# A hybrid decoder block on one core: a seeded accumulation bank, reordered key evacuation, later scaling of probabilities, and more weight tiles in flight

## The chip, the cores and the metric

The kernel runs on one core of one Trainium2 chip. The metric is device time in microseconds (us). Five engines work side by side, each through its own queue in order: TensorE (PE, with PEld for its weight loads), VectorE (DVE), ScalarE (ACT), GpSimd (POOL) and SyncE (SP). In this kernel SP and POOL only issue transfers from device memory, apart from a few fills on POOL. Products land in PSUM, eight banks of 128 x 512 float32. Everything else lies in SBUF.

## The reference, cut to what matters

Sequence 512, model width 1024, float32 throughout.

```
h = rmsnorm(x, norm1_w);  proj = h @ w_in[l]            # rq rk rv rg mq mk mv ga gb
ret = silu(rg) * retention(rotary(rq), rotary(rk)/sqrt(128), rv);  a = ret @ w_ret_out
mq, mk = per-head rmsnorm;  b = moba_attention(mq, mk, mv) @ w_moba_out
x = x + (sigmoid(ga) * a + sigmoid(gb) * b) @ w_o
f = (silu(h2 @ w_ffn_gate) * (h2 @ w_ffn_up)) @ w_ffn_down;  x + f     # h2 = rmsnorm(x, norm2_w), hidden 2816
```

With 512 keys in two blocks of 256 and three selected, the block-sparse attention is the ordinary causal softmax here: eight heads of width 64.

## The kernel before

Every product is made to float32 accuracy out of three passes: each operand is split into a rounded high part and the rest, and `mm3` adds high x high, high x low, low x high. For a weight tile of 128 x 1024 (`raw`) this means one cast on ACT (line 387, `wh<-raw`) and one subtraction on DVE (`wl<-raw,wh`; the helper that records DVE and PE operations is line 217, so their rows all carry L217).

Most of the work is cut into **units** of two output halves by two inner halves, done with seven block products in place of eight (the Winograd form of Strassen's scheme). The weight pieces are called B11, T1, T2, B21, B22, T3, T4, where T1 and T3 are differences that the transfers make, by an accumulating transfer on POOL (line 333) onto a tile that SP has loaded (line 331), and T2 and T4 are further sums: DVE adds them (`raw<-raw,raw`), except that in the units of w_o and of three of the four w_ffn_down parts T4 comes by another accumulating POOL transfer (line 357), which waits until DVE has split T2. The order of a unit is `B11 T1 *1 T2 B21 B22 T3 / T4`: the part behind the slash is put off into the next unit, where `*1` stands. Its banks are X (B11, then T2, T3 and T4 added onto it), Y (T1, B22) and Z (B21). What an `ev` object does with a bank as it goes:

- `p1`: after B11, ACT copies X to SBUF (lines 829 and 1534). T2 may write X only after that.
- `p5`, `u2`: ACT copies of Y and X with the sign turned.
- `c11`: after B21, DVE adds Z and the copy of `p1`: the first quarter of the result. One step later the quarter goes to its consumer (`out`), or in the hidden layer through SiLU on ACT.
- `c12`, `c22`, `c21`: the other quarters.

The banks come from one pool of eight (`main_ps`, `side_ps`), in rotation, for the units and for the side work alike: scores, transposes, values. SBUF tiles of 128 x 1024 come from a pool of 47 (`pairs`), also in rotation, so a tile is handed to its next user in the order in which tiles were given back.

**Order of work.** The emission is written out by hand. Each call of `advance` is a step (about one block of 12 products): first it runs what `later(n, f)` put off by n steps, then it ages the weight splits in flight, then it may start the next one, within a cap (`AHEAD`, `OAHEAD`, `FAHEAD`, `PAHEAD`) and by a running balance of DVE's and PE's load. `run_bg` then does one piece of side work from a list. An arriving weight tile is asked for when an earlier one has been used up (`used` calls `load_w`), so the number in flight stays the same, apart from `EXTRA` (before the values' unit of the attention) and `OEXTRA` (before the unit of w_o), which each add one.

**Stages.** Queries and keys (`tok_double`, four banks each, evacuated by `qk_evac`: copy, square on ACT and sum of squares on DVE, bank by bank; keys in banks 1 and 3 are copied by DVE), then the unit of mv, then gates and retention with the attention as side work (scores, `norm`, transposes, values), the two output branches, w_o, the second norm, and the FFN in four parts of 6, 6, 6 and 4 hidden tiles: units for gate and up, then one for w_ffn_down. The first hidden unit of the FFN is plain (eight products), the second has the order `B11 B21 T1 ...`.

In the attention, `norm` (reciprocal of the row sum and scaling of the probabilities, on DVE) is put off by NLAG = 1 step behind the exponential; the transposes follow four steps behind the scores.

Of the kernel before, what the change touches and what calls it, by code (L numbers as in the profile page):

```python
# [39 lines left out]
EXTRA = 1  # L40
OEXTRA = 1
ORDER = (("rg", 0), ("rk", 0), ("rv", 0), ("gb", 0), ("rk", 1), ("rv", 1), ("rg", 1), ("gb", 1), ("b", 0), ("b", 1), ("ga", 0), ("a", 0), ("ga", 1), ("a", 1))
# [10 lines left out]
ATT = (4, 6)  # L53
NLAG = 1
OAHEAD = (4, 6)
# [109 lines left out]
def hybrid_block(ctx: ExitStack, tc: tile.TileContext, wall, xin, xtok, n2, cin, out):  # L165
# [92 lines left out]
    def later(n, f):  # L258
        later_q.append([n, f])
# [55 lines left out]
    assert not left  # L315
    wstate = {"next": 0, "live": 0, "cap": AHEAD, "load": 0}
    wwait = []
# [20 lines left out]
    def used(r):  # L338

        uses[r] -= 1  # L340
        if not uses[r]:
            del raw[r]
            for f in load_w():
                f()

# [29 lines left out]
    def piece_emit():  # L375
        u, q = r = porder[wstate["next"]]
        wstate["next"] += 1
        wstate["live"] += 1
        fresh = r not in raw
        if fresh:  # L380
            make_sum(u, q)
        w = slice(0, width[r])
        src = raw[r][:, w]

        def high():
            h = big(nm("wh"), F32R)[:, w]
            A.copy(h, src)  # L387
            return h

        def low(h):  # L390
            l = big(nm("wl"), F32R)[:, w]
            V.tensor_tensor(l, src, h.bitcast(F32), ALU.subtract)
            was_split(r)
            return l

        p = Piece(high, low, HLAG if fresh else 0, LLAG)
        pieces[u, q] = p
        wwait.append(p)
# [269 lines left out]
    cur = [0]  # L668

    def tok_double(mov, evac):  # L670

        pss = [main_ps() for _ in range(NT)]
        lows = []
        for k in range(KT):
            for t in range(NT):
                m = ("A11", "A21", "A12", "A22")[k // 4 * 2 + t // 2]
                mm3(pss[t], tuple(x[:, t % 2 * P:t % 2 * P + P] for x in hW(m, k % 4)), mov(k), k == 0, k == KT - 1)
            advance(1)
            for l in lows:
# [78 lines left out]
    def wino_unit(w, ev, hooks={}):  # L758
# [7 lines left out]
        def bank(b):  # L766
            if b not in banks:
                banks[b] = [main_ps(), main_ps()] if wide else main_ps()
            return banks[b]

        def third(x):
            ev.c22(x)
            if "T4w" in order:
                ev.u3(x)

        whole = "T4w" in order
        table = {"B11": ("X", "A11", True, False, ev.p1), "T1": ("Y", "S1", True, False, ev.p5),
                 "T2": ("X", "S2", False, False, ev.u2), "B21": ("Z", "A12", True, True, ev.c11),
                 "B22": ("Y", "S4", False, True, ev.c12), "T3": ("X", "S3", False, whole, third),
# [42 lines left out]
    class Quarters:  # L822
# [4 lines left out]

        def p1(self, x):
            A.copy(self.a[:, :512], x)  # L829

# [6 lines left out]
        def c11(self, z):  # L837
            a = self.a[:, :512]
            V.tensor_tensor(a, z, a, ALU.add)
            later(1, lambda: self.out(0, 0, a))  # L840

# [21 lines left out]
    def qk_evac(i, tiles):  # L863
        def f(t, ps):

            if t % 2 == 0:
                tiles[t], tiles[t + 1] = halves(nm("qk"))
            sq = act(nm("sqh"))
            if i and t % 2:
                V.tensor_copy(tiles[t], ps)  # L870
            else:
                A.copy(tiles[t], ps)
            A.activation(sq, tiles[t] if i else ps, AF.Square)
            V.tensor_reduce(ss[:, i, t, :], sq.rearrange("p (h d) -> p h d", d=MDH), AX.X, ALU.add)
        return f
# [103 lines left out]

    for _ in range(EXTRA):  # L980
        for f in load_w():
            f()
    wino_unit(hW, Quarters(mv_out))


# [85 lines left out]
    def rg_unit(n):  # L1071
        def out(pair, i, x):
            if (pair, i) == (1, 0):
                A.copy(ev.free, x)
                x = ev.free
            srg[2 * n + i, pair] = x
            if (pair, i) == (1, 0):
                gates(n)
                ret_done("rg")

        ev = Quarters(out)
        wino_unit(hW, ev)
# [62 lines left out]
    def rv_out(h0):  # L1145
        def f(pair, i, x):
            rv[h0 + i, pair] = split(f"rv{h0 + i}_{pair}", x, None, 0 if (pair, i) == (1, 0) else SLAG[1])
            if (pair, i) == (1, 0):
# [363 lines left out]
    wstate["cap"] = OAHEAD  # L1512
    for _ in range(OEXTRA):
        for f in load_w():
            f()
    A.activation(warm, warm, AF.Sqrt)
# [8 lines left out]
    class Hidden:  # L1525
# [6 lines left out]

        def p1(self, x):
            A.copy(self.a0, x)

# [6 lines left out]
        def c11(self, z):  # L1542
            V.tensor_tensor(self.a0, z, self.a0, ALU.add)
            later(1, lambda: A.activation(self.a0, self.a0, AF.Silu))

# [64 lines left out]

    wstate["cap"] = FAHEAD
    for c in range(len(CHUNKS)):
        mats = {}
# [83 lines left out]
```

## Time and profile before

| | us |
|---|---|
| median of 3 runs | 813.05 |
| lowest, highest | 810.21, 813.63 |
| the profiled execution | 809.42 |
| its span, first to last instruction | 807.6 |
| PE busy | 783.9 (97%) |
| DVE busy | 659.3 (82%) |
| ACT busy | 438.6 (54%) |
| POOL busy | 64.1 (8%) |

The busy time of an engine is the union of its instructions. Matmuls are pipelined, so one shows 284 ns where the next starts 120 ns later. An idle time in a row of a timeline stands in brackets with what ended it. The share of DMA in a row of windows is the mean over the core's 16 DMA engines.

### The profile page before, as it was taken

How to read it: one execution, taken by the hardware profiler on the slowest of the kernel's cores; microseconds unless marked ns; L12 is line 12 of the kernel's file. 1: busy time of each engine (PE TensorE's matmuls, PEld its weight loads, DVE VectorE, ACT ScalarE, POOL GpSimd, SP SyncE). 2: the span in 40 equal slices, each digit the busy share in tenths (PEclk: the TensorE clock that was granted, in tenths of full speed). 3: DMA queues.
4: the chain of work that ended last, by engine and by line, in shares of the span. 5: the costliest groups of instructions: out<-in, count | busy, mean ns of one | idle time of the engine just before them, and what ended most of it. 6: DMA issues, size and time to landing. Idle time of an engine off the chain costs nothing.

```text
span 807.6 us, 13676 instructions
## 1 busy us (share of the span) xinstructions
PE 783.9 (97%) x5398; PEld 722.5 (89%) x5398; DVE 659.3 (82%) x996; ACT 438.6 (54%) x720; POOL 64.1 (8%) x84
## 2 busy tenths in 40 slices
PE   6998999999999999999999999999999999998997
PEld 5888988888999999998988798988999899987996
DVE  7869878777898678877678998886998798886987
ACT  8546755566537457653545575543555356552641
POOL 0004000000000000000001000011101110020100
PEclk9999999999999999999999999999999999999999
DMA  9742342333527637261798704569837795669702
GB/s 331 229 115 68 105 119 66 75 82 131 130 57 183 151 122 196 90 189 43 244 271 259 182 27 135 138 173 276 211 115 169 216 294 142 157 149 296 177 19 104
DMA packets 38080, 125.95 MB, mean 156 GB/s; under 512 B 4224, under 2 KB 4480, under 8 KB 38016
## 3 DMA queue, kind: packets, MB, share of 16 engines
q1 hardware_dynamic: 28800, 93.88, 33.8%
q0 software_dynamic: 9216, 31.20, 22.5%
q8 instruction: 42, 0.69, 0.3%
q14 instruction: 22, 0.18, 0.1%
HBM read 122.97 MB, written 2.10 MB: 155 GB/s over the span
## 4 chain that ended last, share of the span: by engine, by line
PE 66%; DVE 15%; DMA 7%; issue 7%; ACT 4%; POOL 1%; SPq 0%; ACTq 0%; DVEq 0%; POOLq 0%
PE pm L217 58%; PE ps L217 7%; DMA raw<-wall 7%; DVE wl L217 6%; ACT wh L387 2%; DVE xr L217 2%; DVE raw L217 2%; DVE h L217 1%; DVE ws L217 1%; DVE fb L217 1%; DVE qk L217 0%; ACT p L1007 0%; DVE mx L217 0%; POOL raw L357 0%; DVE gs L217 0%
## 5 line engine op out<-in xcount | busy, mean ns | idle before, releaser
L217 DVE TENSOR_TENSOR wl<-raw,wh 128x1024 fp32r<-128x1024 f32 (+1 forms) x224 | 258.2, 1168 | 44.2 <-ACT wh L387 36.1
L387 ACT CAST wh<-raw 128x1024 fp32r<-128x1024 f32 (+1 forms) x224 | 219.5, 1006 | 104.0 <-DVE raw L217 60.9
L217 PE MATMUL pm<-h,wh 128*128 128x256 f32 x1248 | 226.2, 284 | 3.5 <-ACT h L1467 1.0
L217 PEld LDWEIGHTS pm<-h,wh 128*128 128x128 f32 x1248 | 195.0, 192 | 5.3 <-ACT h L1467 1.2
L217 PE MATMUL pm<-h,wl 128*128 128x256 f32 x624 | 176.8, 283 | 1.1 <-DVE wl L217 1.1
L217 PEld LDWEIGHTS pm<-h,wl 128*128 128x128 f32 x624 | 119.7, 192 | 1.5 <-DVE wl L217 1.5
L333 POOL DMA_DIRECT2D raw<-wall x56 | 49.4, 885 | 636.8 <-DMA raw<-wall 238.9
L217 PE MATMUL pm<-hA,wh 128*128 128x256 f32 x448 | 83.0, 285 | 0.0
L217 PEld LDWEIGHTS pm<-hA,wh 128*128 128x128 f32 x448 | 70.1, 192 | 1.0 <-issue 0.5
L217 PE MATMUL pm<-wh,hA 128*128 128x256 f32 (+1 forms) x304 | 69.1, 310 | 0.0
L217 PE MATMUL pm<-wh,hS 128*128 128x256 f32 x320 | 64.3, 290 | 3.6 <-ACT qa L829 3.6
L217 PE MATMUL pm<-hA,wl 128*128 128x256 f32 x224 | 63.4, 283 | 1.7 <-DVE wl L217 1.7
L217 DVE TENSOR_TENSOR raw<-raw,raw 128x1024 f32<-128x1024 f32 (+1 forms) x48 | 57.0, 1187 | 0.8
L217 PEld LDWEIGHTS pm<-wh,hS 128*128 128x128 f32 x320 | 52.7, 195 | 4.1 <-ACT qa L829 3.8
L217 PEld LDWEIGHTS pm<-wh,hA 128*128 128x128 f32 x304 | 51.0, 191 | 2.5
L217 DVE TENSOR_TENSOR xr<-xr,pm 128x512 f32<-128x512 f32 x74 | 47.0, 679 | 1.3 <-PE pm L217 1.3
L217 PE MATMUL pm<-hS,wh 128*128 128x256 f32 x256 | 47.4, 285 | 0.0
L217 PE MATMUL pm<-wl,hA 128*128 128x256 f32 (+1 forms) x152 | 46.4, 305 | 0.0
L217 PE MATMUL pm<-wl,hS 128*128 128x256 f32 x160 | 45.7, 286 | 0.0
L217 PEld LDWEIGHTS pm<-hA,wl 128*128 128x128 f32 x224 | 42.9, 191 | 1.9 <-DVE wl L217 1.9
L217 PEld LDWEIGHTS pm<-hS,wh 128*128 128x128 f32 x256 | 40.0, 192 | 0.1
L217 PE MATMUL pm<-ret,wh 128*128 128x512 f32 x128 | 39.5, 390 | 0.0
(257 smaller groups left out, 1406.4 us busy)
## 6 DMA issues: line engine op xcount, KB each, us to landing
raw<-wall SPq DMA_DIRECT2D x153, 512.0 KB, 4.6
raw<-wall POOLq DMA_DIRECT2D x55, 512.0 KB, 6.6
raw<-wall SPq DMA_DIRECT2D x23, 256.0 KB, 4.4
raw<-wall POOLq DMA_DIRECT2D x9, 256.0 KB, 6.9
xr<-xtok SPq DMA_DIRECT2D x4, 512.0 KB, 7.9
out<-xr SPq DMA_DIRECT2D x8, 256.0 KB, 2.1
x<-xin SPq DMA_DIRECT2D x7, 256.0 KB, 5.4
cs<-cin SPq DMA_DIRECT2D x1, 512.0 KB, 5.5
```

What stands on the lines that cost most here:

```text
L217: return f(out, *args, **kw)
L333: nc.gpsimd.dma_start(t[:, s], wall[c, :, s], accum_op=ALU.add)
L387: A.copy(h, src)
```

## The change

It has six parts.

1. One bank, `zbank`, is taken out of the rotation for good and serves as Z of every unit (and as the last bank of the queries' product). In units whose order has T1 second and whose products are 256 wide (`seed`), `p1` has ACT copy X into Z instead of into SBUF, and B21 is accumulated onto it. `c11` then has no addition: the consumer reads Z.
2. Following from it, the quarter of `c11` goes out a step earlier, the retention's values are split at once, and the retention gate's unit copies the quarter to SBUF on ACT.
3. `qk_evac` copies all four banks first, and squares the copies after the last.
4. NLAG goes from 1 to 2.
5. `more_raws` replaces the loops that add weight tiles: OEXTRA goes from 1 to 5, and FEXTRA = -2 takes two back at the start of the FFN.
6. A weight piece of at most 512 columns puts its high and low parts in the two halves of one tile of the pool.

```diff
-OEXTRA = 1
+OEXTRA = 5
+FEXTRA = -2
...
-NLAG = 1
+NLAG = 2
...
         if not uses[r]:
             del raw[r]
-            for f in load_w():
-                f()
+            if wstate["drop"]:
+                wstate["drop"] -= 1
+            else:
+                for f in load_w():
+                    f()
+
+    def more_raws(n):
+
+        wstate["drop"] += max(-n, 0)
+        for _ in range(n):
+            if wstate["drop"]:
+                wstate["drop"] -= 1
+            else:
+                for f in load_w():
+                    f()
...
         def high():
-            h = big(nm("wh"), F32R)[:, w]
+            if width[r] <= 512:
+                both.extend(halves(nm("wh"), F32R))
+            else:
+                both.append(big(nm("wh"), F32R))
+            h = both[0][:, w]
...
+    zbank = main_ps()
+
     def tok_double(mov, evac):
 
-        pss = [main_ps() for _ in range(NT)]
+        pss = [main_ps() for _ in range(NT - 1)] + [main_ps() if cur[0] else zbank]
...
+                z = zbank if b == "Z" else main_ps()
+                banks[b] = [z, main_ps()] if wide else z
...
+        def first(x):
+            ev.p1(*([x, bank("Z")] if seed else [x]))
+
         whole = "T4w" in order
+        seed = not wide and order[1] != "B21"
...
-        def p1(self, x):
-            A.copy(self.a[:, :512], x)
+        def p1(self, x, z):
+            A.copy(z, x)
...
         def c11(self, z):
-            a = self.a[:, :512]
-            V.tensor_tensor(a, z, a, ALU.add)
-            later(1, lambda: self.out(0, 0, a))
+            self.out(0, 0, z)
...
             if t % 2 == 0:
                 tiles[t], tiles[t + 1] = halves(nm("qk"))
-            sq = act(nm("sqh"))
             if i and t % 2:
                 V.tensor_copy(tiles[t], ps)
             else:
                 A.copy(tiles[t], ps)
-            A.activation(sq, tiles[t] if i else ps, AF.Square)
-            V.tensor_reduce(ss[:, i, t, :], sq.rearrange("p (h d) -> p h d", d=MDH), AX.X, ALU.add)
+            if t == NT - 1:
+                for x in range(NT):
+                    sq = act(nm("sqh"))
+                    A.activation(sq, tiles[x], AF.Square)
+                    V.tensor_reduce(ss[:, i, x, :], sq.rearrange("p (h d) -> p h d", d=MDH), AX.X, ALU.add)
...
-            if (pair, i) == (1, 0):
-                A.copy(ev.free, x)
-                x = ev.free
+            if i == 0:
+                y = ev.free if pair else ev.a[:, :512]
+                A.copy(y, x)
+                x = y
...
-    for _ in range(OEXTRA):
-        for f in load_w():
-            f()
+    more_raws(OEXTRA)
...
         def c11(self, z):
-            V.tensor_tensor(self.a0, z, self.a0, ALU.add)
-            later(1, lambda: A.activation(self.a0, self.a0, AF.Silu))
+            if not self.whole:
+                V.tensor_tensor(self.a0, z, self.a0, ALU.add)
+                z = self.a0
+            A.activation(self.a0, z, AF.Silu)
...
     wstate["cap"] = FAHEAD
+    more_raws(FEXTRA)
```

## Rows read from the trace of the kernel before

**Rows 1.** PE's waits from 50 to 200 us: total, times, longest

```profile
PE pm L217 <- ACT qa L829: 3.6, 1, 3.6
PE pm L217 <- DVE wl L217: 2.1, 2, 1.7
PE ps L217 <- ACT pt L1039: 0.5, 1, 0.5
```

**Rows 2.** PE's waits from 502 to 790 us

```profile
PE pm L217 <- DVE xr L217: 2.1, 2, 1.9
PE pm L217 <- DVE wl L217: 1.3, 3, 0.8
...
PE pm L217 <- ACT wh L387: 0.5, 1, 0.5
```

**Rows 3.** Windows: stretch, busy time of PE, PEld, DVE, ACT, POOL (instructions), PEclk, DMA share, GB/s

```profile
61.30:65.10 3.80, 0.21 (x2) 0.00 (x1) 2.82 (x5) 3.04 (x5) 0.86 (x1) 0.93 0.30 37
65.10:68.10 3.00, 2.99 (x14) 3.00 (x15) 2.65 (x5) 1.32 (x3) 0.00 (x0) 0.52 0.73 143
68.10:72.00 3.90, 3.90 (x35) 3.90 (x34) 3.69 (x10) 2.79 (x4) 2.08 (x4) 1.00 0.00 0
104.90:106.90 2.00, 0.31 (x3) 0.11 (x2) 1.88 (x4) 0.59 (x3) 0.86 (x1) 1.00 0.51 172
421.00:460.00 39.00, 39.00 (x176) 32.12 (x175) 35.38 (x51) 19.95 (x33) 4.31 (x5) 1.00 0.92 238
```

**Rows 4.** ACT's timeline behind the keys: start, length, instruction [idle before, ended by]

```profile
56.34 0.59 ACT L872 COPY qk<-pm 128x512 f32<-128x512 f32 x1
...
62.06 0.63 ACT L873 ACTIVATE sqh<-qk 128x512 f32<-128x512 f32 x1 [1.35 <-DVE qk L217]
62.60 1.98 ACT L387 CAST wh<-raw 128x1024 fp32r<-128x1024 f32 x2
64.48 0.57 ACT L829 COPY qa<-pm 128x512 f32<-128x512 f32 x1
```

**Rows 5.** DVE's timeline behind the keys

```profile
58.23 0.68 DVE L217 COPY qk<-pm 128x512 f32<-128x512 f32 x1
...
63.66 1.22 DVE L217 TENSOR_TENSOR wl<-raw,wh 128x1024 fp32r<-128x1024 f32 x1 [0.25 <-ACT wh L387]
```

**Rows 6.** DVE's waits, from 62 to 107 us (first row) and from 107 to 200 us (second)

```profile
DVE rl L217 <- ACT p L1007: 3.6, 4, 1.3
...
DVE rl L217 <- ACT p L1007: 14.4, 17, 1.4
```

**Rows 7.** Groups of DVE by form: count, busy us, mean ns, idle before

```profile
L217 DVE TENSOR_TENSOR fa<-pm,fa 128x512 f32<-128x512 f32 x10 | 6.8, 683 | 0.1
...
L217 DVE TENSOR_TENSOR qa<-pm,qa 128x512 f32<-128x512 f32 x9 | 6.1, 682 | 3.5 <-PE pm L217 3.4
```

**Rows 8.** ACT's waits from 502 to 808 us

```profile
ACT wh L387 <- DMA raw<-wall: 28.8, 4, 10.7
```

**Rows 9.** Timelines around the end of the third FFN part: POOL, then ACT

```profile
722.24 0.86 POOL L357 DMA_DIRECT2D raw<-wall  x1 [11.86 <-DVE wl L217]
...
725.18 1.22 POOL L333 DMA_DIRECT2D raw<-wall  x1
...
737.83 2.51 ACT L387 CAST wh<-raw 128x1024 fp32r<-128x1024 f32 x3 [10.68 <-DMA raw<-wall]
```

**Rows 10.** Timelines of ACT and PE in w_o, at the T4 of its unit

```profile
448.57 2.00 ACT L387 CAST wh<-raw 128x1024 fp32r<-128x1024 f32 x2 [3.27 <-DMA raw<-wall]
...
453.86 0.61 PE L217 MATMUL pm<-wh,mx 128*128 128x512 f32 x2
```

**Rows 11.** Timelines of PE and ACT at the tightest use of banks

```profile
165.47 0.48 PE L217 MATMUL ps<-mk3h,mq 128*128 128x512 f32 x1
...
172.76 1.07 PE L217 MATMUL ps<-pt,mv 128*64 128x512 f32 x2
...
172.41 0.56 ACT L1007 ACTIVATE p<-ps,nb,qs 128x256 f32<-128x256 f32 x1
```

More of the change, by code (lines that the diff above doesn't have):

```diff
@@ L315, in hybrid_block @@
     assert not left
-    wstate = {"next": 0, "live": 0, "cap": AHEAD, "load": 0}
+    wstate = {"next": 0, "live": 0, "cap": AHEAD, "load": 0, "drop": 0}
     wwait = []
@@ L383, in piece_emit @@
         src = raw[r][:, w]
+        both = []
         def high():
-            h = big(nm("wh"), F32R)[:, w]
+            if width[r] <= 512:
[3 more added lines that the diff above has]
+            h = both[0][:, w]
             A.copy(h, src)
@@ L390, in low @@
         def low(h):
-            l = big(nm("wl"), F32R)[:, w]
+            l = (both[1] if width[r] <= 512 else big(nm("wl"), F32R))[:, w]
+            both.clear()
             V.tensor_tensor(l, src, h.bitcast(F32), ALU.subtract)
@@ L767, in bank @@
             if b not in banks:
-                banks[b] = [main_ps(), main_ps()] if wide else main_ps()
+                z = zbank if b == "Z" else main_ps()
+                banks[b] = [z, main_ps()] if wide else z
             return banks[b]
@@ L774, in third @@
                 ev.u3(x)
+        def first(x):
+            ev.p1(*([x, bank("Z")] if seed else [x]))
         whole = "T4w" in order
-        table = {"B11": ("X", "A11", True, False, ev.p1), "T1": ("Y", "S1", True, False, ev.p5),
-                 "T2": ("X", "S2", False, False, ev.u2), "B21": ("Z", "A12", True, True, ev.c11),
+        seed = not wide and order[1] != "B21"
+        table = {"B11": ("X", "A11", True, False, first), "T1": ("Y", "S1", True, False, ev.p5),
+                 "T2": ("X", "S2", False, False, ev.u2), "B21": ("Z", "A12", not seed, True, ev.c11),
                  "B22": ("Y", "S4", False, True, ev.c12), "T3": ("X", "S3", False, whole, third),
@@ L978, in mv_out @@
                 bg.append(lambda n=n: att_step(n))
-    for _ in range(EXTRA):
-        for f in load_w():
-            f()
+    more_raws(EXTRA)
     wino_unit(hW, Quarters(mv_out))
@@ L1146, in f @@
         def f(pair, i, x):
-            rv[h0 + i, pair] = split(f"rv{h0 + i}_{pair}", x, None, 0 if (pair, i) == (1, 0) else SLAG[1])
+            rv[h0 + i, pair] = split(f"rv{h0 + i}_{pair}", x, None, 0 if i == 0 else SLAG[1])
             if (pair, i) == (1, 0):
@@ L1512, in hybrid_block @@
     wstate["cap"] = OAHEAD
-    for _ in range(OEXTRA):
-        for f in load_w():
-            f()
+    more_raws(OEXTRA)
     A.activation(warm, warm, AF.Sqrt)
@@ L1531, in __init__, with p1 @@
             self.a0, self.a1, self.b1, self.b0 = (x[:, i:i + 512] for x in (self.a, self.b) for i in (0, 512))
-        def p1(self, x):
-            A.copy(self.a0, x)
+        def p1(self, x, z=None):
+            self.whole = z is not None
+            A.copy(z if self.whole else self.a0, x)
         def p5(self, y):
```

## The prediction

> **What bounds the kernel now.** I read the page first: PE is busy for 783.9 of a span of 807.6 us, so idle PE is 23.7 us in all, of which a start before the first weights and a tail hold some 10. No change of DVE or ACT work can win more than PE's own waits, so the second view is the list of those waits, by stretch, and the third is what stands behind each one. The reader is to see two clusters. In the first [rows 1] one wait of 3.6 us, for ACT's copy of the values' unit, and one of 1.7 us, for a DVE split; between 200 and 421 us there is none. In the FFN [rows 2] there are shorter ones for DVE and ACT. The windows [rows 3] show the price of the long wait beyond itself: granted clock 0.52 in the 3.0 us behind it (the 1.2 GHz level), with 14 matmuls, where the next 3.9 us at 1.00 (2.4 GHz) hold 35. At 35/3.9 the 3.0 us would have held 27; the 13 missing are 1.4 us. The wait at 105 us (1.7 us idle) left the clock at 1.00.
>
> **Part 3, the evacuation of the keys.** PE's wait of 3.6 us ends at 65.1 [rows 1, 3], so T1 is done at 61.5; T2 needs X, which ACT copies at 64.48 only [rows 4]. Ahead of that copy stand two weight casts and the squares, and two of the squares waited 1.35 us each for DVE's copy of the odd banks; the row of the second is shown. DVE's copy at 58.23 [rows 5] stands behind the reduction of the bank before, which waits for ACT's square of it. The two engines hand each other the work bank by bank. After the change DVE copies both odd banks at once (it is idle there), ACT copies two banks from 56.34 and then makes four squares, all at the pitch of the row at 62.06 (0.54 us from its start to the next): six of them end at 59.58. The casts begin there, not at 62.60. The copy of X moves with them by 3.0 us, to 61.46, ends at 62.03, and PE waits about 0.6 us, not 3.6. Saved: **3.0 us**. Waits up to 1.9 us showed no lower clock [rows 2, 3], so the **1.4 us** go too. Bounds: 0 if the copy is held by something else ahead of it, 3.6 + 1.4 if nothing is left. The queries' squares come the same way but PE does not wait for them: nothing, as the four banks of the keys' product are free beside three banks and zbank; without that cover it would be the 1.9 us of four copies.
>
> **Parts 1, 2 and 4, DVE.** Eighteen additions go: all nine of the projections' units and nine of the ten of the hidden layer (the second hidden unit keeps its own), each 0.68 us [rows 7], 12.3 us of DVE. They only count where DVE is late for PE. That is so from 63 to 106 us: DVE has no gap there but its waits for exponentials, 3.6 us in four [rows 6], and ends with the split for which PE waits 1.7 us [rows 1, 3]. What is late next: PE comes there 4.4 us earlier (the sum of part 3), DVE starts its first split 3.0 us earlier (behind the cast, not at 63.66 [rows 5]), does two additions less (1.2 us at the pitch of 0.6 between neighbours) and, with `norm` a step later, finds the exponential done: 3.6 us. That is 7.8 us against the 4.4 + 1.7 = 6.1 us it needs. Saved: **1.7 us**, with 1.7 to spare; the lower bound is 0, if half of the 3.6 us comes back as other waits. From 107 to 200 us the same step gives DVE 14.4 us [rows 6], but PE waits there for 0.9 us only (0.5 for ACT, 0.4 for DVE [rows 1]); I take **0.5**. Behind `norm` on DVE's queue stand weight splits, so these move earlier; the transposes come four steps after the scores, so a step more leaves two.
>
> The copy of X now goes to a bank. No row shows ACT writing to PSUM; between the 0.57 us of the copy to SBUF [rows 4] and nothing lies the gain, and the loss is bounded by a cast of twice the size, half of 1.98 us. I take 0.57, since it is the same instruction but for its target. The Trainium skill (ScalarE: Activation LUTs, in "Step-by-step: what each stage is for") says that ScalarE reaches PSUM faster than SBUF as a destination; by it the copy would be below 0.57 us, and the sum larger by less than 0.1. B21 waits for this copy, but T2, ahead of it, waits for the same one, so PE gets no new wait. The copy waits in turn until the last unit's consumer has read Z: three products earlier, some 8.6 us at 24 matmuls of 0.12 us. The two copies more on ACT in the gate's units lie in its idle time (46% of the span); uncovered they would be 1.2 us.
>
> **Part 5, weight tiles.** In the FFN ACT waits four times for an arriving tile, 28.8 us in all [rows 8], three times at the end of a part. The rows of the third [rows 9] show how: the unit of w_ffn_down keeps the tiles of T2 for T4, no other is given back, so the first tiles of the next part are asked for late; the accumulating transfer at 725.18 also stands on POOL's queue behind the two of line 357, the first of which held the queue for 11.86 us, waiting for DVE. ACT's cast then comes at 737.83, after 10.68 us, DVE's splits behind it, and DVE's addition to the residual behind those, for which PE waits 1.9 us [rows 2]. Two tiles more, in flight through the FFN (five less one less two), replace the two that are held: these two loads are asked for two tiles earlier, some 8 us at the 20 us of a unit's five, and their POOL transfer then stands before those of line 357, not behind. Behind it the line 357 transfer may wait for that tile's landing, and T4 for it; it has the 11.86 us for which POOL stood idle. Of the waits of rows 2 belong to these three places: 2.1 (residual), 1.3 (splits), 0.5 (cast), together 3.9 us; I take **3.4**, as one short split wait lies before the late tile. Bounds: 0 and 3.9.
>
> At w_o four tiles more come at a time when DMA is at 0.92 [rows 3], and there nothing waits on PE. T4 of that unit, by line 357, arrives just in time: ACT waits 3.27 us and casts at 448.57, so that the split (half of 2.00, then 1.22 us as in [rows 5]) ends near 450.8, and PE begins T4 at 453.86 [rows 10]: 3 us to spare. I take nothing, and keep a rival for it. What speaks against it in the Trainium skill (DMA: Bandwidth & Descriptors, "Queues, rings and completion order"): each DMA engine takes turns between the queues that have work, so SP's new loads would slow POOL's accumulating one. No row here has the two cases side by side.
>
> **Part 6** gives each narrow piece one tile, not two, for both parts: no instruction changes. It returns tiles sooner or, as both halves must be done, later; both parts are read by the same product, so nothing either way.
>
> **Sum.** 3.0 + 1.4 + 1.7 + 0.5 + 3.4 = 10.0 us. Against the profiled execution's own 809.4 (span 807.6 and 1.8 around it) that is 799.4. That execution ran 3.6 us below the median of 813.05; against the median it is **803.0**. By the bounds: nothing, or 3.6 + 1.4 + 1.7 + 0.9 + 3.9 = 11.5, which is 801.5; the runs themselves lie 3.4 us apart.
>
> **Rivals.** *DVE is still late at 105 us.* The waits for exponentials come back in other places, since the chain from maximum to exponential to scaling is as long as before. Then 1.7 + 0.5 is not won: 805.3. Against it: the reciprocal waits for ACT while splits stand ready behind it [rows 6].
>
> *The transfers give nothing.* Line 357 and bandwidth set the FFN's arrivals, and at w_o four tiles, by five loads in seven transfers of 512 KB some 2.9 MB, at 238 GB/s [rows 3] are 12 us of transfers, of which half ahead of T4 would use up its 3 us and cost 3 more: 813.05 - 6.6 + 3 = 809.5, about no change. For it: 0.92 of DMA. Against it: POOL waited for DVE there, not for DMA.
>
> *Seven banks are too few (slower).* Place: the attention, 93 to 195 us, with 24 score tiles. A score tile written at 165.47 is read until 172.97 (the exponential at 172.41 and its 0.56 [rows 11]), and at 172.76, when the values open theirs, I count two X, three score tiles, two transposed ones and the new one: eight without Z. With seven PE would wait 0.2 us there. If instead each score found no bank for 0.85 us, it would be 24 x 0.85 = 20.4: 813.05 - 10.0 + 20.4 = 823.5. It decides from (10.0 + 4.1) / 24 = 0.6 us each. Against it: the tile is held that long because DVE and ACT are late there, and DVE gets 14.4 us back [rows 6].
>
> *The copy of X does not move.* The casts wait for their tile, not for the squares; then 3.0 + 1.4 fall away: 807.5. Against it: the two casts run without idle time before them [rows 4].
>
> **How the numbers follow.** A measurement of this kernel tells about 0.5%, 4.1 us, from no change: 809 and 817.1 are the borders. Forecast 0.62 (own range 799 to 807), DVE still late 0.12, the copy not moved 0.04: all faster, 0.78. Transfers 0.13: same. Too few banks 0.09: slower. The low end, 797, is 801.5 less what a run may lie below the median (2.8 us at the lowest) and a little for waits not counted here; the high end, 811, takes in all but the slower case and the upper part of the transfers'.
>
> **What would show it.** Right: PE's wait for the copy of X below 1 us and no stretch at 0.5 of the clock behind it; none at 105 us; DVE's waits for exponentials below 4 us; ACT's waits for arriving tiles below 8 us in the FFN and no PE wait over 0.5 us at the ends of its parts; 18 DVE additions fewer. Wrong: a PE wait for a score's bank, one in w_o for T4, or ACT's copy to a bank clearly above 0.6 us.

## The result, and the profile after

| | before | after |
|---|---|---|
| median of the runs, us | 812.42 (4 runs, 810.21 to 813.63) | 800.94 (4 runs, 800.27 to 801.35) |
| profiled execution, us (span) | 809.42 (807.6) | 800.78 (798.7) |
| mean granted clock of the profiled execution | 0.998 | 0.997 |

The ratio is 0.9861 (95%: 0.9837 to 0.9885): faster, by 11.5 us between the medians and by 8.6 us between the two profiled executions. The forecast was 10.0 us less: 803.0 by the median, which the result undercuts by 2.1 within its range of 797 to 811, and 799.4 by the profiled execution. The page of the changed kernel:

```profile
span 798.7 us, 13670 instructions
...
PE 782.8 (98%) x5398; PEld 722.8 (90%) x5398; DVE 648.9 (81%) x978; ACT 439.8 (55%) x722; POOL 64.1 (8%) x84
...
PE 84%; DVE 8%; ACT 4%; issue 2%; DMA 2%; POOL 0%; SPq 0%; DVEq 0%; ACTq 0%; POOLq 0%
```

DVE has its 18 instructions and 10.4 us less, ACT two copies more. PE is busy for 1.1 us less, and the other 7.8 of the 8.9 us that the span is shorter are PE's idle time. That idle time is in the list of PE's waits, here from 50 to 200, 200 to 421, 421 to 502 and 502 to 790 us (total, times, longest):

```profile
PE pm L218 <- ACT pm L859: 0.4, 1, 0.4
...
PE pm L218 <- DVE qb L218: 1.8, 1, 1.8
...
PE pm L218 <- ACT h L1496: 1.3, 1, 1.3
PE pm L218 <- ACT fa L1562: 0.9, 1, 0.9
PE pm L218 <- ACT fa L1565: 0.8, 1, 0.8
PE pm L218 <- DVE h L218: 0.3, 1, 0.3
...
PE pm L218 <- DVE wl L218: 0.2, 1, 0.2
```

The first line answers to [rows 1], the last to [rows 2]: 3.6, 2.1 and 0.5 us have become 0.4, and 2.1, 1.3 and 0.5 us have become 0.2. The second line is new; nothing of the sort stood between 200 and 421 us before.

The windows (columns as in [rows 3]): behind the values' copy the clock is whole, w_o is as full of transfers as it was, and behind the second norm there is now a stretch at 0.50, the 1.2 GHz level:

```profile
63.10:66.10 3.00, 3.00 (x25) 3.00 (x26) 2.64 (x5) 1.35 (x3) 0.86 (x1) 1.00 0.23 26
...
416.00:454.00 38.00, 38.00 (x169) 31.31 (x168) 34.02 (x49) 18.71 (x30) 4.38 (x5) 1.00 0.94 247
...
459.60:462.60 3.00, 3.00 (x15) 3.00 (x15) 2.71 (x5) 2.59 (x6) 0.00 (x0) 0.50 0.00 0
```

A list of waits does not say what a wait was worth. PE makes the same 5398 matmuls in the same order of products in both kernels and in every experiment, so they can be counted, and the start of the n-th one compared. The table is worked out from the traces, one profiled execution of each kernel; the column `before` is the start itself, the others the difference to it, in us (e1 to e12 are the experiments below; e8 is left out, as it follows the changed kernel within 0.3 us):

```
   n  before after   e1    e2    e3    e4    e5    e6    e7    e9   e10   e11   e12
   0    6.3  +0.1  +0.0  -0.0  +0.0  +0.0  +0.0  +0.1  +0.1  +0.0  +0.1  +0.0  +0.0
 150   40.6  +1.1  +0.2  +0.7  +1.3  +0.8  +0.0  +0.1  +1.3  +1.1  +0.4  -0.0  +0.8
 300   69.8  -3.3  -4.2  +0.9  +1.5  +1.0  -4.4  -4.3  -3.1  -3.3  -4.0  +0.0  -3.7
 600  108.8  -4.8  -2.9  +0.1  +1.3  -0.8  -4.7  -5.8  -4.6  -4.8  -3.9  -1.9  -5.2
1350  208.2  -7.1  -2.9  -0.1  +1.3  -3.1  -7.0  -8.1  -6.9  -7.1  -4.2  -4.2  -7.5
1500  226.2  -5.0  -2.9  +1.9  +1.3  -3.1  -7.0  -8.1  -4.8  -7.1  -2.1  -0.7  -5.4
3000  452.3  -5.0  -2.8  +2.0  +1.4  -3.0  -6.7  -8.1  -4.8  -7.1  -2.1  -0.7  -5.4
3150  475.4  -3.2  -1.0  +1.5  +3.6  -0.7  -5.2  -7.9  +1.1  -7.6  -1.5  +1.4  -3.1
3600  532.4  -3.2  -1.0  +1.5  +3.6  -0.7  -5.1  -7.8  +1.0  -6.5  -1.4  +1.5  -3.1
4500  669.9  -5.7  +0.6  +4.0  +1.1  +0.8  -7.7 -10.3  -1.3  -9.0  -4.0  -1.1  -5.6
5100  758.0  -8.4  +0.2  +3.9  -1.6  +2.1 -10.4 -13.0  -3.9 -11.7  -6.7  -3.7  -8.3
5397  803.2  -8.6  +0.2  +3.7  -1.6  +2.2 -10.4 -13.3  -4.2 -12.0  -7.0  -4.0  -8.6
```

Read the steps down a column. After: 1.1 us lost before matmul 150 (the start, which differs between executions of any of these kernels), 4.4 won at the values' copy, 1.5 by matmul 600, 2.3 by 1350, then 2.1 lost, 1.8 lost at the second norm, and 5.2 won in the FFN.

### The profile page after: what moved, and what is told of

It reads as the page before. It is cut to its first block, busy times and chain, and to the rows that moved or that the text cites. A ratio compares the mean times of both kernels' runs of the same rounds, so it can differ in the third digit from the quotient of the medians.

```text
span 798.7 us, 13670 instructions
## 1 busy us (share of the span) xinstructions
PE 782.8 (98%) x5398; PEld 722.8 (90%) x5398; DVE 648.9 (81%) x978; ACT 439.8 (55%) x722; POOL 64.1 (8%) x84
## 4 chain that ended last, share of the span: by engine, by line
PE 84%; DVE 8%; ACT 4%; issue 2%; DMA 2%; POOL 0%; SPq 0%; DVEq 0%; ACTq 0%; POOLq 0%
PE pm L218 76%; PE ps L218 8%; DVE wl L218 2%; ACT wh L407 2%; DMA raw<-wall 2%; DVE xr L218 1%; DVE raw L218 1%; DVE ws L218 1%; DVE h L218 1%; DVE fb L218 1%; DVE gs L218 1%; DVE gsl L218 0%; ACT f L1508 0%; ACT h L1496 0%; DVE xn L218 0%
## 5 line engine op out<-in xcount | busy, mean ns | idle before, releaser
L218 DVE TENSOR_TENSOR wl<-raw,wh 128x1024 fp32r<-128x1024 f32 x203 | 245.1, 1220 | 44.7 <-ACT wh L407 34.7
L218 PE MATMUL pm<-wh,gsh 128*128 128x512 f32 x112 | 39.9, 391 | 0.2
```

The lines of the kernel that those rows point to most:

```text
L218: return f(out, *args, **kw)
```

## The experiments

Each was timed in rounds beside the kernel before on the same chip; the ratio is to that kernel's runs.

| run | what differs | median, us | ratio, 95% |
|---|---|---|---|
| e1 | before + keys' order | 807.32 | 0.9945 [0.9927, 0.9963] |
| e2 | before + sums on PE | 812.60 | 1.0007 [0.9990, 1.0025] |
| e3 | before + tiles | 807.51 | 0.9947 [0.9928, 0.9965] |
| e4 | before + later scaling | 806.16 | 0.9942 [0.9920, 0.9965] |
| e5 | after - sums on PE | 798.85 | 0.9844 [0.9816, 0.9871] |
| e6 | after, additions still counted | 796.63 | 0.9810 [0.9786, 0.9835] |
| e7 | after, no piece begun at the end of w_o | 804.12 | 0.9899 [0.9878, 0.9920] |
| e8 | after - shared tile of narrow weights | 800.49 | 0.9856 [0.9831, 0.9881] |
| e9 | e6, one piece begun at the end of w_o | 797.21 | 0.9824 [0.9798, 0.9850] |
| e10 | after - later scaling | 803.12 | 0.9894 [0.9870, 0.9919] |
| e11 | after - keys' order | 805.45 | 0.9917 [0.9893, 0.9941] |
| e12 | after, tiles +2 instead of +4 - 2 | 797.90 | 0.9837 [0.9809, 0.9864] |

### One part alone on the kernel before

**e1, the keys' banks copied first.**

```
-            sq = act(nm("sqh"))
...
-            A.activation(sq, tiles[t] if i else ps, AF.Square)
-            V.tensor_reduce(ss[:, i, t, :], sq..., AX.X, ALU.add)
+            if t == NT - 1:
+                for x in range(NT):
+                    sq = act(nm("sqh"))
+                    A.activation(sq, tiles[x], AF.Square)
+                    V.tensor_reduce(ss[:, i, x, :], sq..., AX.X, ALU.add)
```

> The kernel before with the keys' banks all copied first, and nothing else of the change. Theory A (the squares stood ahead of the casts and of the copy of X on ACT): PE's wait for the copy of X falls from 3.6 to about 0.6 us and no stretch behind it stands at half the clock, 4.4 us in all; but PE then reaches the split at 105 us 4.4 us earlier and DVE only 3.0 us earlier, so the wait there grows from 1.7 to about 3.1 us. Net 3.0 us less, ratio 0.996. Rival B (the wait went because the copy of X now goes to a bank and not into a tile): the wait of 3.6 us stays and the time is that of before, ratio 1.000. Rival C (DVE at 105 us takes nothing back): 4.4 us less, ratio 0.9945.

The copy still goes to a tile here, and PE's wait for it is 0.4 us all the same: B falls. The column of e1 has A's sizes: 4.4 us won by matmul 300 (from +0.2 to -4.2), 1.3 given back by 600, 3.1 left against 3.0 expected; C falls by that column. The place is another than A's: the wait at 105 us stays at 1.8 us, and 1.0 of the 1.3 us goes between 84 and 89 us, at an earlier split, where the list has a new wait of 0.5 us. The ratio lies at C's figure; in it stands the clock of e1's runs too, 0.996 to 1.000 against 0.993 to 0.998 of before, of which the last section tells. The column then loses 1.9 us at the second norm, where the clock falls, and 1.2 in the FFN, which is told behind e4.

**e2, the sums of C11 on PE.** The bank `zbank` and the edits to `first`, `p1`, `c11` and their two consumers, as in the diff, and nothing else.

> The kernel before with the sums of C11 made by PE in a bank of its own, and nothing else of the change. Theory A (DVE work counts only where PE waits for DVE): 18 additions, 12.3 us of DVE, are gone, but the wait of 3.6 us for the copy of X stays; the one at 105 us shrinks by the 1.2 us of two additions; the FFN's waits stay, since late tiles make them. About 1 us less, ratio 0.998 to 1.000. Rival B (less DVE work shortens the FFN's waits as well, since DVE's additions there stand ahead of its splits): 3 us less, ratio 0.996. Rival C (seven banks are too few where the kernel holds scores and transposes): PE waits for banks between 93 and 195 us, ratio above 1.003.

A, or less than A: 10 us of DVE work are gone and the time is that of before. 0.8 us are won at 105 us, then 2.0 are lost between matmuls 1350 and 1500, where PE waits 1.8 us for `qb` as in the changed kernel. The wait that is new in the changed kernel belongs to this part. PE has no wait for a bank between 93 and 195 us: C falls.

**e3, more tiles for arriving weights.**

```
-OEXTRA = 1
+OEXTRA = 5
+FEXTRA = -2
```

with `more_raws` and the count `drop`, as in the diff.

> The kernel before with more tiles for arriving weights from w_o on, and nothing else of the change. Theory A (the tiles that are held through the unit of w_ffn_down delay the next part's loads): ACT's waits for arriving tiles in the FFN fall from 28.8 to below 10 us, and PE's waits for the splits, the cast and the residual there, 3.9 us, go to below 0.5; ratio 0.9955. Rival B (the extra tiles must be paid for: without narrow weights sharing a tile the pool of 47 is short in w_o): PE waits in w_o or at the second norm by 1 us or more, and the gain is half or less, ratio 0.998 to 1.003. Rival C (bandwidth sets the arrivals): ACT waits as long as before, ratio 1.000.

A: ACT's waits for arriving tiles from 502 us on are 5.4 us in four, the longest 1.6, against 28.8 [rows 8]; the column wins 5.2 us between matmuls 3600 and 5100. The wait for h at the second norm is 1.7 us, 0.7 more than before, and the column loses 2.2 us there, which is B's sign; but e1 and e4, which have no tiles more, wait 1.5 and 1.8 us, so it does not tell for B, nor is B excluded there. C falls.

**e4, the scaling a step later.**

```
-NLAG = 1
+NLAG = 2
```

> The kernel before with the scaling of the probabilities a step later, and nothing else of the change. Theory A: DVE's waits for exponentials fall from 3.6 (62 to 107 us) and 14.4 (107 to 200 us) to below 3 and 6 us, the wait at 105 us shrinks by what DVE gains ahead of it, up to 1.7 us, and nothing else moves; 1 to 2 us less, ratio 0.998. Rival B (the waits come back in the chain from the maximum to the exponential): DVE's idle time in those stretches and PE's wait at 105 us stay as they are, ratio 1.000. Rival C (the transposes find the scaling late): a new PE wait for DVE's scaling between 93 and 195 us, ratio above 1.001.

Better than A. PE waits for nothing between 66 us and the second norm, and the column wins 1.8 us by matmul 600 and 2.3 more by 1350, where A had nothing. Most of the second gain is at the values of one pair of heads, at 172 us of before, on PE's timeline (start, length, instruction, count, idle time before):

```profile
172.76 1.07 PE L217 MATMUL ps<-pt,mv 128*64 128x512 f32 x2
174.32 2.37 PE L217 MATMUL ps<-pt,mv 128*64 128x512 f32 x14 [0.48 <-ACT pt L1039]
176.61 0.50 PE L217 MATMUL pm<-hA,wh 128*128 128x256 f32 x2
```

and on that of e4:

```profile
171.89 2.38 PE L217 MATMUL ps<-pt,mv 128*64 128x512 f32 x16
174.19 0.50 PE L217 MATMUL pm<-hA,wh 128*128 128x256 f32 x2
```

The same 16 matmuls take 3.85 us from first start to the next product before, and 2.30 in e4. 1.55 us were lost, and the trace calls only 0.48 of them idle. The two matmuls of the row of 1.07 us start 0.5 us apart, where in e4 the first two start together; a single one is 0.6 us long in both traces, so that delay counts as busy. The 14 behind take 2.29 us before and 1.82 in e4. The list of waits that the forecast used showed 0.9 us for this stretch, and the counted matmuls show 2.3. DVE's waits for exponentials fell as A said, to 2.6 and 5.5 us from 3.6 and 14.4.

The end of e4's column, +2.2, is not what the part is worth: this execution took 811.53 us, and the other seven 804.75 to 807.90. It loses 2.3 us at the second norm and 2.9 in the FFN, with half the clock behind a wait in both places.

**What e1, e2 and e4 have in common.** Each of them loses 1.6 us at one place in the FFN. At the end of the second part PE waits for DVE's addition to the residual; PE's row there before, and in e1:

```profile
653.20 0.47 PE L217 MATMUL pm<-wh,g 128*128 128x512 f32 x1 [0.27 <-DVE xr L217]
```

```profile
653.83 0.47 PE L217 MATMUL pm<-wh,g 128*128 128x512 f32 x1 [1.87 <-DVE xr L217]
```

In e2 and e4 it waits 1.86 us. What is late is an arriving tile: its accumulating transfer on POOL landed 10.2 us after its issue before, and 12.1 to 12.5 us after it in these three. Why it takes longer there stays open. With the tiles of part 5 (e3 and the changed kernel) PE does not wait at this place. So a part alone loses something that the whole change does not, and the three runs are no clean measure of what their parts are worth in it.

### One part taken out of the changed kernel

**e10, the scaling back at one step** (`NLAG = 1`), **and e11, the keys' banks one by one** (the edit of e1 undone).

> The changed kernel with the scaling of the probabilities back at one step. Theory A (the forecast's sum at 105 us: 6.1 us needed, of which 4.2 come from the earlier split and the two additions, 3.6 from the later scaling): PE waits 1.9 us there, and the waits between 107 and 200 us, 2.3 us by the matmuls' numbers, return; about 4 us above the changed kernel, ratio to before 0.991. Rival B (the 12.3 us less of additions are enough by themselves): no wait at 105 us over 0.5, within 1 us of the changed kernel, ratio 0.987.

> The changed kernel with the keys' banks copied and squared one by one as before. Theory A (order on ACT): PE waits 3.6 us for the copy of X again, half the clock behind it in most executions, and nothing else changes since DVE gains as much as PE loses; 3.2 + 1.4, 4.6 us above the changed kernel, ratio to before 0.992. Rival B (other parts have already made the copies earlier): within 1.5 us of the changed kernel, ratio 0.988 or less.

In e10 PE waits 1.4 us for the split at 105 us, against A's 1.9, and 0.4 for one at 186. Between matmuls 300 and 1350 its column wins 0.2 us, where that of the changed kernel wins 3.8: 3.6 lost against A's 4.2, by A's mechanism. The time is not 4 us above the changed kernel but 1.5 to 2.7 (the middle of five runs is 802.43, the ratio 0.0033 higher; a sixth run took 2087 us, stands in the table's median and is in neither of these). Between the two profiled executions it is 1.6, since e10 starts 0.7 us earlier and loses 1.2 us less at the second norm; its runs keep a mean clock of 0.998 to 0.999, where the changed kernel's have 0.997. e11 shows A's wait: PE waits 3.6 us for the copy of X, half the clock stands behind it (0.50 from 66 to 68 us), and matmul 300 is where it was before. That it ends 4.5 us above the changed kernel, A's figure, is in part luck: its execution also loses 1.4 us to a lower clock behind the wait at 210 us (last section), and starts 1.1 us earlier.

**e5, the sums of C11 back on DVE.** The edits of e2 undone, all else of the change left in.

> The changed kernel without the sums of C11 on PE: DVE adds them as in the kernel before, all eight banks are free, the rest of the change is in. Theory A (12.3 us less DVE work are off the path everywhere, and what that part does to the order brings the new wait of 1.8 us at 205 us): that wait is gone, no other comes, the wait at 105 us stays at nothing because the later scaling and the earlier copies cover it; 799 us, 2 us below the changed kernel, ratio to before 0.984. Rival B (the additions count now that PE waits for little else): waits for DVE at 105 us and in the FFN return, 2 us or more above the changed kernel, ratio 0.989 or more.

A in the main: the wait at 205 us is gone, and the median is 2.1 us below that of the whole change. The two ratios' intervals overlap, and of the 1.8 us between the two profiled executions 1.1 are the start. B has a part: short waits for splits (0.4 and 0.2 us) are back, and between matmuls 300 and 600 the column wins 0.3 us, where that of e6 (below) wins 1.5.

### The new wait at 205 us

The waiting matmul needs X, which DVE frees with `qb<-qa,pm`. DVE's timeline in the changed kernel:

```profile
206.08 0.62 DVE L218 SCALAR_TENSOR_TENSOR sc<-ps,sk,sc 128x384 fp32r<-128x384 f32 x1 [4.32 <-ACT sc L1220]
206.62 0.68 DVE L218 TENSOR_TENSOR qb<-qa,pm 128x512 f32<-128x512 f32 x1
```

DVE stands for 4.32 us behind a score that ACT has not scaled. ACT's timeline:

```profile
188.85 1.05 ACT L407 CAST wh<-raw 128x1024 fp32r<-128x1024 f32 x1
190.59 0.58 ACT L1220 ACTIVATE sc<-ps,sk 128x384 fp32r<-128x384 f32 x1 [0.69 <-DVE dia L218]
191.63 1.05 ACT L407 CAST wh<-raw 128x1024 fp32r<-128x1024 f32 x1 [0.46 <-PE pm L218]
...
198.03 1.04 ACT L407 CAST wh<-raw 128x1024 fp32r<-128x1024 f32 x1
...
205.47 0.58 ACT L1220 ACTIVATE sc<-ps,sk 128x384 fp32r<-128x384 f32 x1 [5.77 <-PE pm L218]
```

PE had begun to write the score's bank at 196.99. What ACT waits for (5.77 us) is a matmul of the unit (`pm`), which does not write the score: the reading is that the tile for the scaled score is the one that this matmul's weight gives back, as all 47 tiles are taken. The trace has no addresses and does not show that itself; e6 tests what follows from it. The program's list of work begins a weight's split early when it has counted less DVE work than PE work; the 18 additions are no longer in the count.

**e6, the additions still counted.**

```
         def c11(self, z):
+            dve_cost(512)
             self.out(0, 0, z)
...
                 z = self.a0
+            else:
+                dve_cost(512)
             A.activation(self.a0, z, AF.Silu)
```

> The changed kernel whose work list still counts each addition that fell away as DVE work when it decides how early a weight is split; no instruction is added or removed, only their order. Theory A (the wait of 1.8 us at 205 us comes because a weight is split one piece earlier and holds the tile that a score needs): the wait goes, the time falls by 1.8 to 2.0 us, ratio to before 0.984. Rival B (the wait comes from the bank that is set aside, or from results that are handed on a step earlier): the wait stays, ratio 0.986.

A. PE, DVE and ACT have as many instructions as in the changed kernel; ahead of this score one weight is cast later (three more in the FFN, where the column moves as before), and the same row reads in e6:

```profile
198.21 0.58 ACT L1221 ACTIVATE sc<-ps,sk 128x384 fp32r<-128x384 f32 x1 [1.96 <-PE pm L218]
```

ACT waits 1.96 us there, PE not at all, and the column loses nothing between 1350 and 1500. The median falls by 4.3 us, more than the 2.1 of the wait. Of the 4.7 us between the two profiled executions 1.6 come at the second norm, where this kernel keeps its clock (0.999 to 1.000 over all five runs), and 1.0 are the start. So the wait's 2.1 us are what the trace gives to the count; PE's wait at the norm is as long as in the changed kernel (1.2 against 1.3 us), and that the count keeps the clock there is not shown. By the median e6 is the fastest version of the study.

### The second norm

ACT's timeline in the changed kernel has two weight casts ahead of the norm's first copy, whose transposes PE began at 454.50:

```profile
454.69 1.99 ACT L407 CAST wh<-raw 128x1024 fp32r<-128x1024 f32 x2
456.58 0.58 ACT L1508 COPY f<-ps 128x512 f32<-128x512 f32 x1
457.06 0.58 ACT L1496 CAST h<-ps 128x512 fp32r<-128x512 f32 x1
```

**e7, no piece begun in the last product of w_o**, on the changed kernel, **and e9, one piece begun instead of two**, on e6.

```
-    wino_unit(mx, Residual(squares))
+    wino_unit(mx, Residual(squares), {"T3": lambda: wstate.update(cap=(2, 2))})
```

(in e9 the cap is (3, 3)).

> The changed kernel with no new weight piece begun during the last product of w_o, so that two casts of 1.99 us in all no longer stand on ACT ahead of the second norm's copies. Theory A (PE's wait of 1.28 us for the norm's h is those two casts, and the granted clock of 0.50 behind it, from 460 to 462 us, comes from that wait): h is ready 1.5 us earlier, PE waits for it below 0.3 us, the clock stays at 1.00 there; 1.3 + 0.3 + about 1.5 of clock, 3 us less than the changed kernel, ratio to before 0.9825. Rival B (the norm waits for its chain of squares and scaling, or the split of h on DVE is the next to be late): 0.5 us less or nothing, ratio 0.986.

Neither: the wait for ACT's h is gone, as A has it (0.8 us for DVE's split of h is left), but the run is 3.2 us slower than the changed kernel. PE's and DVE's timelines of e7:

```profile
467.70 0.58 PE L218 MATMUL pm<-h,wl 128*128 128x256 f32 x1 [3.93 <-DVE wl L218]
```

```profile
463.77 2.74 DVE L218 SCALAR_TENSOR_TENSOR xn<-xr,r_y,n2r 128x512 f32<-128x512 f32 x4
466.43 4.62 DVE L218 TENSOR_TENSOR wl<-raw,wh 128x1024 fp32r<-128x1024 f32 x4
```

The piece that was begun later has its split behind the whole norm of the lower rows on DVE's queue, and PE waits 3.93 us for it, with half the clock for nearly 6 us behind that (0.50 from 468 to 472 us, 0.61 from 472 to 474).

> The run with the counted additions, and in the last product of w_o one weight piece begun instead of two: one cast of 1.0 us on ACT and one split of 1.2 us on DVE stand ahead of the second norm's copies and splits, the other piece follows behind them and its split behind the scaling of the lower rows. Theory A (the 3.9 us of the run that begun none came from the split that then stood behind the lower rows' norm, not from the casts): PE's wait for h falls from 1.2 to about 0.3 us, no wait for a weight's split over 0.5 us comes, 0.9 us less than that run, ratio to before 0.980. Rival B (the moved split is late again): a new wait of 1 us or more for a split at 465 to 470 us, ratio 0.982 or more.

A on the mechanism, and nothing gained. The waits of PE from 421 to 502 us in e9:

```profile
PE pm L218 <- ACT fa L1563: 1.9, 1, 1.9
PE pm L218 <- ACT fa L1566: 0.8, 1, 0.8
PE pm L218 <- ACT h L1497: 0.4, 1, 0.4
PE pm L218 <- DVE h L218: 0.3, 1, 0.3
```

The wait for h is 0.4 us, not 1.2, and that for the first hidden unit's copy is 1.9, where e6 has 0.9: what is won at the norm goes back some microseconds later. The two runs' times overlap (796.66 to 797.83, and 795.80 to 797.22).

### Tiles

**e8, two tiles for a narrow weight again** (`wh` and `wl` from `big`, as before), **and e12, two tiles more and none taken back** (`OEXTRA = 3`, `FEXTRA = 0`).

> The changed kernel with two tiles again for the parts of a narrow weight, high and low apart. Theory A (the forecast's: no instruction changes, and the tiles come back soon enough): the time of the changed kernel, within 1 us, ratio to before 0.986. Rival B (the sharing pays for the additional tiles of arriving weights): the pool of tiles is short, casts or loads wait for tiles, new waits of PE of 2 us or more, from w_o on above all, ratio 0.989 or more.

> The changed kernel with two more tiles for arriving weights from w_o on and none taken back, where the change has four more and takes two back at the FFN. Theory A (the two that stay through the FFN do the work): waits for arriving tiles in the FFN as in the changed kernel, 7.9 us in four, and its time within 1 us, ratio to before 0.986. Rival B (the two that w_o has on loan bring its weights earlier): ACT's wait of 3.3 us at w_o's last product grows and PE waits at the second norm a microsecond longer or more, ratio 0.988 or more.

e8 is A: 0.4 us from the changed kernel, as the forecast had part 6. e12 has 11.5 us of waits for tiles on ACT in the FFN, in five, against 7.9, but PE waits for none of them, and its profiled column ends where that of the changed kernel does: the two tiles that stay do the work. Of B's signs ACT's wait for the last tile at w_o is 2.8 us, not above 3.3, and the wait for h at the second norm is 2.0, against 1.3. Its runs fall in two groups, 797.42 to 797.90 with a mean clock of 1.000 and 800.04 to 800.50 with 0.997 and 0.998; so the median of 797.9 goes with the clock, and does not say what two tiles are worth.

## Why the forecast came out as it did

**Part 3 was right in mechanism and size.** ACT's timeline of the changed kernel answers to [rows 4]:

```profile
57.48 1.08 ACT L899 COPY qk<-pm 128x512 f32<-128x512 f32 x2
58.44 2.21 ACT L903 ACTIVATE sqh<-qk 128x512 f32<-128x512 f32 x4
60.53 2.00 ACT L407 CAST wh<-raw 128x1024 fp32r<-128x1024 f32 x2
62.42 0.60 ACT L859 COPY pm<-pm 128x512 f32<-128x512 f32 x1
```

This execution is 1.1 us late from its start. From the first copy to the first cast it takes 3.05 us (3.24 in the forecast), and to the copy of X 4.94 (5.12); PE then waits 0.4 us (0.6). 3.2 us of wait and the lower clock are the 4.4 us of the column, as 3.0 + 1.4 had it. e1 and e11 show that the order does it, and not where the copy goes.

**The wait at 105 us: the size held (1.5 by the column, 1.7 forecast), its working did not.** The forecast wanted 6.1 us and had 7.8, of them 3.6 from waits for exponentials. Only 1.0 of these went (3.6 to 2.6). What helped beside is order: before, a reciprocal with its wait and a scaling stand ahead of the split; after, they stand behind it. DVE's timeline of before, then of after:

```profile
104.99 0.16 DVE L217 RECIPROCAL rl<-l 128x1 f32<-128x1 f32 x1 [0.29 <-ACT p L1007]
105.19 0.42 DVE L217 TENSOR_SCALAR p<-p,rl 128x384 f32<-128x384 f32 x1
105.53 1.22 DVE L217 TENSOR_TENSOR wl<-raw,wh 128x1024 fp32r<-128x1024 f32 x1
```

```profile
100.13 0.68 DVE L218 TENSOR_TENSOR qb<-qb,pm 128x512 f32<-128x512 f32 x1
100.73 1.22 DVE L218 TENSOR_TENSOR wl<-raw,wh 128x1024 fp32r<-128x1024 f32 x1
101.86 0.68 DVE L218 TENSOR_REDUCE mx<-ps 128x1 f32<-128x512 f32 x1
102.58 0.16 DVE L218 SCALAR_TENSOR_TENSOR nb<-mx,qs 128x1 f32<-128x1 f32 x1
102.66 0.15 DVE L218 RECIPROCAL rl<-l 128x1 f32<-128x1 f32 x1
```

Reciprocal and scaling are 0.5 us (104.99 to 105.53), and the 0.29 us of waiting is in the 1.0. DVE's first split came 3.2 us earlier, not 3.0. So 3.2 + 1.2 + 1.0 + 0.5 = 5.9, about the 6.1 wanted, with nothing to spare where the forecast had 1.7: the split ends at 101.95, and the matmul that needs it starts at 102.05. With the two additions back (e5 against e6) 1.2 us are lost again, with the scaling back at one step (e10) 1.5 at this place. "DVE has no gap there but its waits for exponentials" was a misreading: DVE has 1.7 us of other waits between 62 and 107 us, for a square, casts and a root. It does not change the sum, as 0.8 of them lie behind the first split and 0.6 are still there after the change.

**From 107 to 200 us the term was mis-sized**: 0.5 forecast, 2.3 measured, for the reason shown with e4. The step that failed is "PE waits there for 0.9 us only": that list counts only what the trace calls idle. The starts of the matmuls show the rest.

**The FFN's term was mis-sized too**: 3.4 forecast, 5.2 by the column, for waits that [rows 2] put at 3.9. Five waits of 3.75 us in all went, and by the matmuls' starts each cost 0.2 to 0.5 us more than listed (the one for the residual 2.1, listed 1.86), which is 1.4: a matmul's row is 0.28 us long where the next starts 0.12 later, so the beginning of a wait counts as busy. The forecast had also set off 0.5 for a short wait, and of the short ones only 0.2 stayed. The criterion of ACT's waits for tiles, below 8 us, is met with 7.9. The transfers' rival does not come true: ACT waits 3.33 us for the last tile at w_o, where it waited 3.27 [rows 10], at 247 GB/s, and POOL's transfers of 512 KB take a median of 6.9 us to land, 6.6 before. The rule that was weighed against it (the Trainium skill, DMA: Bandwidth & Descriptors, "Queues, rings and completion order": each DMA engine takes turns between queues) is not contradicted, but no delay of the accumulating transfer by the added loads shows in that row.

**Parts 1 and 2 are worth nothing here, or a little less**, which the forecast had not seen: the additions won 0.8 us in e2 and 1.2 in e6 against e5, and the wait at 205 us cost 2.0. By the medians the loss is not clear of noise. "They only count where DVE is late for PE" was right for the instructions; it left out what their missing count does to the order of the work. That they help once the count is kept is shown by e6 against e5, 1.2 us between matmuls 300 and 600. (The 18 additions took 10.4 us off DVE's busy time, not 12.3, as neighbours overlap: the pitch is 0.6.) ACT's copy into a bank costs what the one into a tile cost: 587 and 572 ns (lines 859 and 1562), against 586 and 580 before. The Trainium skill (ScalarE: Activation LUTs, "Step-by-step: what each stage is for") has ScalarE faster towards PSUM; at this shape the runs do not show it. No wait for a bank appeared, so the rival of the seven banks falls.

**What the forecast's list of signs missed**: DVE's waits for exponentials are 2.6 and 4.9 us, not below 4 in all, and yet the time came. They were a poor sign, since most of them were not on the path.

**The sum, and luck.** Between the profiled executions the change won 8.6 us, less than the forecast's 10.0: the two sizes that were too small give 1.8 + 1.8 more, the wait at 205 us and the second norm take 2.1 + 1.8, the start 1.1. So the sum came near because 3.6 us that it missed stood against 5.0 us of losses that it did not have, and that is luck. Between the medians it is 11.5. The profiled execution of before had a mean clock of 0.998, that is 0.002 x 807.6 = 1.6 us below full speed; over the 25 runs of before that e1 to e4 were compared with, the middle is 0.996, 3.2 us, and the range 0.993 to 0.998. So a typical run of before loses 1.6 us more to the clock than the one that the sum was made against, which also has one of the earliest starts of the profiled executions (last section). That is part of the 2.9 us between 8.6 and 11.5; the rest is open.

## What to carry to other kernels

Count the instructions of the engine that bounds the kernel and compare when the n-th one starts: waits that the trace books as busy time show there, and so does the place where a gain is given back. When work is taken from an engine whose load a planner counts, the plan changes with it: here a weight was split one piece too early and held a tile that a score needed, so that 10 us less work on DVE won 1 us and lost 2, and the lines that keep the count won the 2 us back. A cast that seems to stand in the way may carry a split that must stand ahead of something else: moving it cost 3.2 us, and moving half of it only moved the wait.

## What the runs showed of the hardware

The granted clock falls behind some waits of PE and not behind others of the same length. The wait of 3.6 us behind the values' unit was followed by 0.50 to 0.58 over 2 us in every profile that has it (before, e2, e3, e4, e11). The waits of 1.86 us for the residual left it whole at 745 us of before and at 654 us of e4, and were followed by 0.50 at 745 us of the same execution of e4 and by 0.53 to 0.62 at 656 us of e2. The wait of 1.8 us at 205 us left the clock at 1.00 in the changed kernel, and was followed in e11 by these rows:

```profile
210.00:212.00 2.00, 1.77 (x12) 1.78 (x13) 1.64 (x5) 1.14 (x4) 0.00 (x0) 0.85 0.00 0
212.00:214.00 2.00, 2.00 (x12) 2.00 (x11) 1.49 (x3) 0.63 (x1) 0.00 (x0) 0.50 0.00 0
214.00:216.00 2.00, 2.00 (x15) 2.00 (x15) 0.04 (x1) 0.16 (x1) 0.00 (x0) 0.79 0.65 221
```

At the second norm waits of 0.95 (before), 0.50 (e2), 1.2 (e6) and 1.6 us (e10) left it whole, and waits of 1.2 (e5), 1.3 (after), 1.5 (e1), 1.6 (e11), 1.7 (e3), 1.8 (e4, e8) and 2.0 us (e12) were followed by a stretch at 0.50. In the two profiled executions that wait about as long, e6 and the changed kernel, having it or not is 1.6 us. The middles of e12's two groups are 2.5 us apart (797.75 and 800.27), of which the mean clocks, 1.000 and 0.997 or 0.998, make some 2; where it fell in the runs without a profile is not on record. The forecast's sentence that waits up to 1.9 us show no lower clock was true of the one execution it was read from. What decides between two such waits stays open; no run here was made for it.

The start differs as well: matmul 150 starts at 40.6 us in before and e5 and at 41.7 in the changed kernel and e9, with the same work ahead of it. From 10 to 12 us PE made 10 matmuls in the one and 7 in the other. The windows give a clock of 1.00 for both, but they count a stretch without a record as whole: the clock's records in the traces begin at 10.0 us in before and e5, at 12.3 in the changed kernel and 12.4 in e9. PE's rows show what stands ahead of that. In before, then in the changed kernel:

```profile
10.08 0.63 PE L217 MATMUL pm<-mh,hA 128*128 128x512 f32 x2
10.54 0.40 PE L217 MATMUL pm<-ml,hA 128*128 128x512 f32 x1
```

```profile
10.23 1.06 PE L218 MATMUL pm<-mh,hA 128*128 128x512 f32 x2
11.09 0.63 PE L218 MATMUL pm<-ml,hA 128*128 128x512 f32 x1
```

From the first row to the second two matmuls take 0.46 us in before and 0.86 in the changed kernel, about twice as long: PE is at the 1.2 GHz level there, and 2.3 us more of it make the start 1.1 us later. In each of the profiled executions matmul 150 is late by half of the time by which its clock records begin later than those of before, within 0.1 us. When the clock first rises differs between executions, from 10.0 to 12.8 us; what sets it is open.
